# Second product of the score matmuls over 128 rows instead of 64, in a hybrid four-layer decoder step

## The chip, the cores and the metric

The kernel runs on one core of one Trainium2 chip. The metric is the device time of one execution in microseconds (us), as the median over runs of the whole program. A core has a matrix engine (TensorE; "PE" in the profile, its weight loads "PEld"), VectorE ("DVE"), ScalarE ("ACT"), GpSimd ("POOL"), and SyncE ("SP"), which issues most of the DMAs. Each engine works off its own queue in order, and waits for others through semaphores.

## The reference

One inference step of a decoder trunk with four layers, for 512 prompt tokens (one sequence) and 32 sample tokens (8 sequences of 4), width 1024. Every layer is `x = x + mixer(rmsnorm(x)); x = x + conv_ffn(rmsnorm(x))`. The mixers are mLSTM in layers 0 and 3, gated linear attention (GLA) in layer 1, and sliding-window softmax attention with sinks in layer 2. All arrays are float32. What matters here are the two score products of the prompt tokens:

```python
# mLSTM, 8 heads, keys and queries of 64
qk = jnp.einsum('bthd,bshd->btsh', q, k) * w          # w: causal decay
num = jnp.einsum('btsh,bshv->bthv', qk, v) + ...

# softmax attention, 16 query heads on 4 key heads of 64, window 128
s = jnp.einsum('bnqkgd,bnrkd->bnkgqr', q, k) * (HDC ** -0.5)
s = jnp.where(mask[None, :, None, None], s, NEG)
p = jax.nn.softmax(jnp.concatenate([s, sink], axis=-1), axis=-1)[..., :-1]
return jnp.einsum('bnkgqr,bnrkd->bnqkgd', p, v)
```

The rest are projections, the convolutional feed-forward (2816 wide), GLA, the decode paths of the sample tokens, and the new states that are returned.

## The kernel before, in words

**Precision.** Large products are made on operands of the type `F32R` ("fp32r" in the profile). Each operand is split into a high half (a copy to F32R, `hi`) and a low half (`src - hi`, `lo`), and a product is hi·hi + hi·lo + lo·hi. The weights come from HBM in units of up to four 128x128 blocks (`wr`). ScalarE makes `wh` (line 191) and VectorE `wl` (line 192), up to three units or more ahead of use, from a ring of six buffers each.

**Order of the work.** A kernel-wide list of units fixes the order of the projections (`gemm` for outputs with features on partitions, `group` for V). Attention runs beside it as generators (`push`): `gemm` calls `tick` after each 128-row block of its contraction, which lets a generator emit its next piece. So the score products of attention stand in TensorE's queue between the products of the projections. A scheduler behind the program then orders each engine's queue by priority and by estimated readiness, and that order is fixed when the program runs. Nearly every product is issued by the helper `mm` (line 164), so rows of the profile are told apart by their tiles.

**mLSTM scores.** A head has 64 features, and two heads share a tile `Q[p]`, `K[p]` of 128 partitions. `prep(h)` builds for head h three tiles of 128 partitions, `ks`, `qs` and `ql`, one buffer each, where `r` are the 64 rows in which the head lies and `o` the other 64:

- `ks[r]` = high half of k (ScalarE, line 716), `ks[o]` = low half of k (VectorE, 719);
- `qs[r]` and `qs[o]` = high half of q, twice (ScalarE, 717 and 718);
- `ql[r]` = low half of q (VectorE, 720); `ql[o]` is not written.

`scores(h)` then makes for each of four blocks of 128 keys a first product over all 128 rows, `ks·qs` = hi·hi + lo·hi at once, with 512, 384, 256 or 128 query columns, and adds a second one over the 64 rows `r`, hi·`ql`. VectorE multiplies the result by the decay, and `av(h)` uses it. `prep(h + 1)` and the decays of the next head are emitted before `av(h)`, and `scores(h + 1)` after it.

**Softmax scores.** The other way round: here q is split into two halves of the partitions (`qa`, `qb` = tag `qs`: the high half of a head in its own 64 rows, the low half in the other 64; line 1435 on ScalarE, 1436 on VectorE), and k is held twice: `KE` has the high half of the even key head in both halves of the partitions, `KO` that of the odd one (four copies on ScalarE). `KL` has the low half of the even head in rows 0 to 63 and of the odd one in rows 64 to 127 (lines 1418 and 1419 on VectorE). `scores` makes for each of two query blocks a first product over 128 rows, q·`KE` or q·`KO`, and adds one over the 64 rows `hr` of the head, q_hi·`KL`, all with 256 key columns. A head takes 8 products, in two PSUM tiles. Then come the masked maximum (VectorE, line 1472), the exponentials (ScalarE, 1476), the scaling (`normalise`, 1502 on VectorE and 1504 on ScalarE), transposes on TensorE (`transp`, line 167) and the product with V (`pv`).

**The convolution's state.** `ffn` holds its old and new state in a tile `cc` (176 KB are loaded into it at its start, line 424) in the pool of the layer's mixer, with the tag `x1`. The softmax layer's pool also has `kc`, one buffer for the cached keys of the decode path: `load_kc(0)` fills it at the start and `load_kc(1)` again after the first `decode`.

Of the kernel before, what the change touches and what calls it, by code (L numbers as in the profile page):

```python
# [10 lines left out]
F32 = mybir.dt.float32  # L11
F32R = mybir.dt.float32r
I32 = mybir.dt.int32
AF = mybir.ActivationFunctionType
ALU = mybir.AluOpType
AX = mybir.AxisListType
PSUM = bass.MemoryType.PSUM
# [3 lines left out]
NP = 512  # L21
# [9 lines left out]
XW = NF * 34  # L31
# [81 lines left out]
class Step:  # L113
# [35 lines left out]
        self.defer = []  # L149
        self.credit = 0.0  # L150

# [1 line left out]
    def t(self, n=562, p=128, dt=F32):  # L153
        return self.tp.tile([128, 562], dt, tag="t", name="t")[0:p, 0:n]

# [10 lines left out]
    def tr(self, out, in_, k):  # L166
        self.nc.tensor.transpose(out, in_, self.ident[0:k, 0:k])  # L167

# [1 line left out]
    def wdma(self, upto):  # L170
        while self.n_dma < min(upto + 1, len(self.units)):
            u = self.n_dma
# [29 lines left out]
        self.n_use += 1  # L202
        return [(hi[:, i * w:(i + 1) * w], lo[:, i * w:(i + 1) * w]) for i in range(len(kts))]

# [1 line left out]
    def adv(self, q, amount):  # L206
        q[0][1] -= amount
        while q and q[0][1] <= 0:
# [50 lines left out]
        while len(self.defer) > 1:  # L259
            self.adv(self.prio, 1)  # L260

# [1 line left out]
    def gemm(self, mat, kts, c0, hi, lo, evac, off=0):  # L263
        kts = list(kts)
        self.room()
# [83 lines left out]
    def h2(self, ap):  # L349
        return ap.rearrange("p (a b) -> p a b", a=2)  # L350

# [1 line left out]
    def xprep(self, kt, gcol, parts="ab"):  # L353
        nc = self.nc
        x = self.XT[:, kt]
# [59 lines left out]

        self.push(gen(), prio=True, delay=0.01)

# [1 line left out]
    def ffn(self, L, last):  # L419
        nc, a = self.nc, self.a  # L420
        cc = self.mp.tile([128, XW], F32, tag="x1", name="cc")
        cin = cc[:, 0:NF * 16].rearrange("p (f b w) -> p f b w", f=NF, b=NB)
        cout = cc[:, NF * 16:NF * 34].rearrange("p (f x) -> p f x", f=NF)
        nc.sync.dma_start(out=cin, in_=a["fst"][L].rearrange("p (f b w) -> p f b w", f=NF, b=NB))
        rb = self.RB

        def dec(ap):
            return ap.rearrange("p (b x) -> p b x", b=NB)

        for ci, ch in enumerate(CHUNKS):  # L430
            for n, f in enumerate(ch):
                pw = P_CW + (L * NF + f) * 3
                pb = P_CB + L * NF + f
                g = self.t()
                nc.gpsimd.memset(g[:, 0:2], 0.0)
                nc.gpsimd.tensor_copy(dec(g[:, 514:562])[:, :, 0:2], cin[:, f])
                s2 = self.t(T)

                def gate(acc, g=g, s2=s2, f=f, pw=pw, pb=pb):
                    nc.vector.tensor_tensor(out=g[:, 2:274], in0=acc[:, 0, 0:HT], in1=rb[:, 0:HT], op=ALU.mult)  # L440
                    nc.vector.tensor_tensor(out=g[:, 274:514], in0=acc[:, 1, 0:240], in1=rb[:, HT:NP], op=ALU.mult)  # L441
                    nc.vector.tensor_tensor(out=dec(g[:, 514:562])[:, :, 2:6], in0=dec(acc[:, 1, 240:272]), in1=dec(rb[:, NP:T]), op=ALU.mult)  # L442
                    nc.gpsimd.tensor_copy(cout[:, f, 0:2], g[:, 512:514])  # L443
                    nc.gpsimd.tensor_copy(dec(cout[:, f, 2:18]), dec(g[:, 514:562])[:, :, 4:6])
                    c = self.t(560)
                    nc.scalar.activation(c, g[:, 2:562], AF.Identity, scale=self.par[:, pw + 2:pw + 3], bias=self.par[:, pb:pb + 1])  # L446
                    nc.vector.scalar_tensor_tensor(out=c, in0=g[:, 1:561], scalar=self.par[:, pw + 1:pw + 2], in1=c, op0=ALU.mult, op1=ALU.add)
                    nc.vector.scalar_tensor_tensor(out=c, in0=g[:, 0:560], scalar=self.par[:, pw:pw + 1], in1=c, op0=ALU.mult, op1=ALU.add)
                    nc.scalar.activation(c, c, AF.Silu)
                    nc.vector.tensor_tensor(out=s2[:, 0:NP], in0=c[:, 0:NP], in1=rb[:, 0:NP], op=ALU.mult)  # L450
                    nc.vector.tensor_tensor(out=dec(s2[:, NP:T]), in0=dec(c[:, 512:560])[:, :, 2:6], in1=dec(rb[:, NP:T]), op=ALU.mult)

                def up(acc, s2=s2, n=n):
                    h = self.t(T)
                    nc.vector.tensor_tensor(out=self.h2(h), in0=acc[:, :, 0:HT], in1=self.h2(s2), op=ALU.mult)  # L455
                    self.split(self.HH[:, n], self.HL[:, n], h)

                self.gemm(f"fu{L}", range(KT), 128 * f, self.XH, self.XL, gate)
                self.gemm(f"fu{L}", range(KT), 128 * (NF + f), self.XH, self.XL, up)
            fin = ci == len(CHUNKS) - 1  # L460
            for mt in range(6 if last and fin else 8):
                self.gemm(f"fd{L}", ch, 128 * mt, self.HH, self.HL,
                          lambda acc, mt=mt: self.resid(mt, acc, (P_GM + 8 * (L + 1) if not last else None) if fin else -1))
        nc.sync.dma_start(out=a["f_o"][L], in_=cout.rearrange("p f x -> p (f x)"))
# [78 lines left out]
        nc.vector.tensor_scalar(out=u, in0=u, scalar1=1.0 / n, scalar2=EPS, op0=ALU.mult, op1=ALU.add)  # L543
        nc.gpsimd.tensor_tensor(out=u, in0=u, in1=self.half[0:p, 0:cols], op=ALU.pow)  # L544

# [1 line left out]
    def mlstm(self, L, j):  # L547
        nc, a, tc = self.nc, self.a, self.tc
        ctx = ExitStack()
# [161 lines left out]
        def prep(h):  # L711
            r = slice(64 * (h % 2), 64 * (h % 2) + 64)
            o = slice(64 - 64 * (h % 2), 128 - 64 * (h % 2))
            q, k = Q[h // 2][r, 0:NP], K[h // 2][r, 0:NP]
            ks, qs, ql = [mp.tile([128, NP], F32R, tag=x, name=x) for x in ("ks", "qs", "ql")]
            nc.scalar.activation(ks[r], k, AF.Copy)
            nc.scalar.activation(qs[r], q, AF.Copy)
            nc.scalar.activation(qs[o], q, AF.Copy)
            nc.vector.tensor_tensor(out=ks[o], in0=k, in1=ks[r].bitcast(F32), op=ALU.subtract)
            nc.vector.tensor_tensor(out=ql[r], in0=q, in1=qs[r].bitcast(F32), op=ALU.subtract)  # L720
            KQ[h] = (ks, qs, ql, r)

        def scores(h):
            ks, qs, ql, r = KQ.pop(h)
            ws = SW[h]
            s23 = None
            for i in range(4):
                n = NP - 128 * i
                if i < 2:
                    s = self.m()[:, 0:n]  # L730
                elif i == 2:
                    s23 = self.m()
                    s = s23[:, 0:256]
                else:
                    s = s23[:, 256:384]
                self.mm(s, ks[:, i * 128:(i + 1) * 128], qs[:, i * 128:NP], True, False)
                self.mm(s, ks[r, i * 128:(i + 1) * 128], ql[r, i * 128:NP], False, True)
                nc.vector.tensor_tensor(out=ws[i], in0=s, in1=ws[i], op=ALU.mult)

        def hnorm(num, den, ss, em, sc, cols, p, tag):  # L740
            # num: list of PSUM [p, 128], den: SBUF [p, cols]
            nc.vector.scalar_tensor_tensor(out=sc, in0=den, scalar=-1.0, in1=den, op0=ALU.mult, op1=ALU.max)
            nc.vector.tensor_tensor(out=sc, in0=sc, in1=em, op=ALU.max)
            nc.vector.reciprocal(out=sc, in_=sc)
            for c, x in enumerate(num):
                junk = self.junk[0:p, 0:128]
                nc.scalar.activation(junk, x, AF.Square, accum_out=ss[:, c:c + 1])
            nc.vector.tensor_tensor(out=ss, in0=ss, in1=sc, op=ALU.mult)
            nc.vector.tensor_tensor(out=ss, in0=ss, in1=sc, op=ALU.mult)
            self.rms_scale(ss, 128, cols, p)  # L750
            nc.vector.tensor_tensor(out=sc, in0=sc, in1=ss, op=ALU.mult)
# [225 lines left out]
        self.outproj(f"aw{j}", L)  # L977
        return ctx

# [1 line left out]
    def gla(self, L):  # L981
        nc, a, tc = self.nc, self.a, self.tc
        ctx = ExitStack()
# [378 lines left out]
        self.outproj("bw", L)  # L1362
        return ctx

# [1 line left out]
    def swa(self, L):  # L1366
        nc, a, tc = self.nc, self.a, self.tc
        ctx = ExitStack()
# [3 lines left out]
        KF = mp.tile([128, 2, T], F32, name="KF")  # L1372
        KE = mp.tile([128, 2, NP], F32R, name="KE")
        KO = mp.tile([128, 2, NP], F32R, name="KO")
        KL = mp.tile([128, 2, NP], F32R, name="KL")
        KC = {}

        def load_kc(kvp):
# [30 lines left out]
        def kevac(m):  # L1409
            def f(acc):  # L1410
# [4 lines left out]
                nc.scalar.activation(KE[64:128, m], x[0:64, 0:NP], AF.Copy)  # L1415
                nc.scalar.activation(KO[0:64, m], x[64:128, 0:NP], AF.Copy)
                nc.scalar.activation(KO[64:128, m], x[64:128, 0:NP], AF.Copy)
                nc.vector.tensor_tensor(out=KL[0:64, m], in0=x[0:64, 0:NP], in1=KE[0:64, m].bitcast(F32), op=ALU.subtract)
                nc.vector.tensor_tensor(out=KL[64:128, m], in0=x[64:128, 0:NP], in1=KO[64:128, m].bitcast(F32), op=ALU.subtract)
            return f  # L1420

        def qevac(m):
# [30 lines left out]
        def scores(m, par, pr, st):  # L1453
            kvp, g = m // 4, m % 4
            head = (2 * kvp + par) * 4 + g
            q = QS[m][par]
            hr = slice(64 * par, 64 * par + 64)
            ks = KO if par else KE
            s = self.m().rearrange("p (a x) -> p a x", a=2)
            for i in range(2):  # L1460
                blk = 2 * pr + i
                k0 = max(0, blk - 1) * 128
                t0 = blk * 128
                self.mm(s[:, i], q[:, t0:t0 + 128], ks[:, kvp, k0:k0 + 256], True, False)
                self.mm(s[:, i], q[hr, t0:t0 + 128], KL[hr, kvp, k0:k0 + 256], False, True)
            sm = mp.tile([128, 2, 256], F32, tag="smx", name="smx", bufs=6)
            mx, ng, su, es = st
            sink = sk[:, head:head + 1]
# [144 lines left out]
        self.outproj("cw", L)  # L1613
        return ctx

# [1 line left out]
    def run(self):  # L1617
        nc, a = self.nc, self.a
        nc.vector.memset(self.half, -0.5)
# [186 lines left out]
```

## Time and profile before

| | |
|---|---|
| time, median of 3 runs | 2652.68 us (2652.5 to 2652.69) |
| profiled execution: span on the core | 2653.1 us |
| mean granted TensorE clock of the profiled execution | 0.994 of full |
| products (TensorE instructions) | 21303 |
| ScalarE, VectorE instructions | 2096, 3455 |

The span of the profiled execution is its own time; it lies 0.4 us above the median of the other runs. A row of a view of groups reads: line, engine, operation, tile written <- tiles read, shape, x count | busy us, mean ns of one | idle us of the engine before them, and what ended that idle time. For a product the two numbers "128*128" or "64*128" ahead of the shape are the rows and columns of TensorE's array that it uses, and the shape is that of the operand that streams. A row of a view of one tile gives the least, median and largest duration in ns, and the start of the first and the last one in us. A row of the timeline gives start and duration in us, and at its end how many like it are merged. A row of the view by windows gives the stretch, its length, the busy time of PE, PEld, DVE, ACT and POOL with counts, the granted TensorE clock, the DMA engines' busy share and GB/s.

### The profile page before, as it was taken

The numbers are of one execution on the slowest core, as the hardware profiler recorded it, in microseconds if no ns is written. First come the engines' busy times: TensorE is split into PE (matmuls) and PEld (weight loads), VectorE is DVE, ScalarE is ACT, GpSimd is POOL, SyncE is SP. The second block draws the span as 40 slices with busy tenths as digits, with TensorE's granted clock in tenths as the row PEclk, the third lists the DMA queues.
The fourth block names the chain that finished last, engine by engine and source line by source line (L and its number), as shares of the span: only waits on it lengthen the run. The fifth ranks groups of instructions, "written<-read, shape, count | busy, mean of one in ns | idle before, by whom it ended". The sixth has DMA issues, their size and how long they took to land.

```text
span 2653.1 us, 52983 instructions
## 1 busy us (share of the span) xinstructions
PE 2627.2 (99%) x21303; PEld 2535.3 (96%) x21303; DVE 1605.4 (61%) x3455; ACT 1105.3 (42%) x2096; POOL 200.4 (8%) x545
## 2 busy tenths in 40 slices
PE   8999999999999999999999999999999999999998
PEld 8999999999998899999998899999999989999998
DVE  5567765645457667464556666364555676756464
ACT  5444433334455543232346554232345444423232
POOL 1000000001012200000010000000010000000000
PEclk9999999999999999999999999999999999999999
DMA  4332333333222224433331123333233322333332
GB/s 171 95 89 76 85 114 94 91 91 99 76 81 89 87 84 148 138 85 92 107 92 51 53 68 88 88 87 90 85 106 90 85 80 80 102 107 96 89 87 80
DMA packets 136294, 245.16 MB, mean 92 GB/s; under 512 B 16272, under 2 KB 32144, under 8 KB 136016
## 3 DMA queue, kind: packets, MB, share of 16 engines
q1 hardware_dynamic: 134608, 240.16, 30.7%
q8 instruction: 168, 2.75, 0.4%
q10 hardware_dynamic: 1440, 1.60, 0.2%
q14 instruction: 78, 0.64, 0.1%
HBM read 228.80 MB, written 14.94 MB: 92 GB/s over the span
## 4 chain that ended last, share of the span: by engine, by line
PE 96%; DVE 2%; ACT 1%; issue 0%; POOL 0%; DMA 0%; DVEq 0%; SPq 0%; ACTq 0%
PE acc L164 81%; PE m L164 14%; PE m L167 1%; POOL s L544 0%; DVE wl L192 0%; DVE t L513 0%; DMA XT<-in_x 0%; DVE t L1068 0%; ACT wh L191 0%; DVE bc L1047 0%; DVE st L831 0%; ACT smx L1476 0%; DVE t L1072 0%; DVE HL L344 0%; POOL sr L1345 0%
## 5 line engine op out<-in xcount | busy, mean ns | idle before, releaser
L191 ACT ACTIVATE wh<-wr 128x512 fp32r<-128x512 f32 (+2 forms) x776 | 482.6, 623 | 1104.4 <-PE acc L164 1019.3
L164 PE MATMUL acc<-XH,wh 128*128 128x272 f32 x3744 | 789.3, 292 | 0.0
L164 PE MATMUL acc<-XH,wl 128*128 128x272 f32 x3744 | 781.1, 289 | 0.0
L164 PE MATMUL acc<-XL,wh 128*128 128x272 f32 x3744 | 778.0, 289 | 0.0
L192 DVE TENSOR_TENSOR wl<-wr,wh 128x512 fp32r<-128x512 f32 (+2 forms) x776 | 523.4, 675 | 326.0 <-ACT wh L191 322.0
L164 PEld LDWEIGHTS acc<-XH,wh 128*128 128x128 f32 x3744 | 588.5, 189 | 9.8 <-issue 6.1
L164 PEld LDWEIGHTS acc<-XL,wh 128*128 128x128 f32 x3744 | 590.0, 189 | 2.6 <-issue 1.6
L164 PEld LDWEIGHTS acc<-XH,wl 128*128 128x128 f32 x3744 | 588.4, 189 | 2.9 <-issue 1.6
L164 PE MATMUL acc<-HH,wh 128*128 128x272 f32 x1920 | 403.7, 290 | 0.0
L164 PE MATMUL acc<-HH,wl 128*128 128x272 f32 x1920 | 399.4, 288 | 0.0
L164 PE MATMUL acc<-HL,wh 128*128 128x272 f32 x1920 | 399.0, 288 | 0.0
L164 PEld LDWEIGHTS acc<-HH,wh 128*128 128x128 f32 x1920 | 302.1, 188 | 2.3 <-issue 1.0
L164 PEld LDWEIGHTS acc<-HL,wh 128*128 128x128 f32 x1920 | 302.4, 188 | 0.0
L164 PEld LDWEIGHTS acc<-HH,wl 128*128 128x128 f32 x1920 | 301.4, 189 | 0.8 <-issue 0.4
L530 DVE TENSOR_TENSOR XT<-acc,XT 128x544 f32<-128x544 f32 x158 | 114.3, 723 | 142.0 <-PE acc L164 141.0
L443 POOL COPY cc<-t 128x2 f32<-128x2 f32 x88 | 54.6, 621 | 1299.2 <-DVE t L441 1294.0
L440 DVE TENSOR_TENSOR t<-acc,rb 128x272 f32<-128x272 f32 x88 | 38.9, 442 | 142.8 <-PE acc L164 140.1
L164 PE MATMUL m<-wh,XH 128*128 128x256 f32 (+1 forms) x400 | 116.2, 291 | 6.8 <-ACT XH L346 6.4
L164 PE MATMUL m<-wl,XH 128*128 128x256 f32 (+1 forms) x400 | 114.9, 288 | 1.0 <-DVE wl L192 1.0
L164 PE MATMUL m<-wh,XL 128*128 128x256 f32 (+1 forms) x400 | 114.9, 288 | 0.0
L455 DVE TENSOR_TENSOR t<-acc,t 128x544 f32<-128x544 f32 x88 | 63.7, 723 | 68.7 <-PE acc L164 68.1
L446 ACT ACTIVATE t<-t,par 128x560 f32<-128x560 f32 x88 | 75.4, 856 | 50.8 <-DVE t L442 50.8
(342 smaller groups left out, 2664.9 us busy)
## 6 DMA issues: line engine op xcount, KB each, us to landing
wr<-in_w SPq DMA_DIRECT2D x700, 256.0 KB
wr<-in_w SPq DMA_DIRECT2D x64, 192.0 KB
st<-in_a_cs SPq DMA_DIRECT2D x16, 520.0 KB
sd<-in_b_s SPq DMA_DIRECT2D x32, 256.0 KB
out_a_cso<-st SPq DMA_DIRECT2D x8, 520.0 KB
na<-scr SPq DMA_DIRECT2D x16, 256.0 KB
out_b_so<-sd SPq DMA_DIRECT2D x16, 256.0 KB
wr<-in_w SPq DMA_DIRECT2D x12, 272.0 KB
```

The source lines that it names most:

```text
L164: self.nc.tensor.matmul(out, lhsT=lhsT, rhs=rhs, start=start, stop=stop, skip_group_check=True, **kw)
L167: self.nc.tensor.transpose(out, in_, self.ident[0:k, 0:k])
L191: self.nc.scalar.activation(hi[:, 0:n], raw[:, 0:n], AF.Copy)
L192: self.nc.vector.tensor_tensor(out=lo[:, 0:n], in0=raw[:, 0:n], in1=hi[:, 0:n].bitcast(F32), op=ALU.subtract)
L440: nc.vector.tensor_tensor(out=g[:, 2:274], in0=acc[:, 0, 0:HT], in1=rb[:, 0:HT], op=ALU.mult)
L443: nc.gpsimd.tensor_copy(cout[:, f, 0:2], g[:, 512:514])
L446: nc.scalar.activation(c, g[:, 2:562], AF.Identity, scale=self.par[:, pw + 2:pw + 3], bias=self.par[:, pb:pb + 1])
L455: nc.vector.tensor_tensor(out=self.h2(h), in0=acc[:, :, 0:HT], in1=self.h2(s2), op=ALU.mult)
L530: self.nc.vector.tensor_tensor(out=self.h2(x), in0=acc[:, :, 0:HT], in1=self.h2(x), op=ALU.add)
```

## The change

The second product of each pair reads all 128 rows. For that its low half is laid into both halves of the partitions: in mLSTM ScalarE copies `ql[r]` to `ql[o]` (one copy of 64x512 a head); in the softmax layer `KL` is replaced by `KEL` and `KOL`, whose own half VectorE writes as before, and whose other half ScalarE copies (two copies of 64x512 for each of two tiles of key heads). The sums gain the term lo·lo, which was left out. To make room for the additional tile, `cc` takes the tag `kc` in the softmax layer. The numbers and sizes of the products stay, apart from the rows that they read.

```diff
@@ ffn
-        cc = self.mp.tile([128, XW], F32, tag="x1", name="cc")
+        cc = self.mp.tile([128, XW], F32, tag="kc" if L % 3 == 2 else "x1", name="cc")
@@ mlstm, prep
             nc.vector.tensor_tensor(out=ql[r], in0=q, in1=qs[r].bitcast(F32), op=ALU.subtract)
-            KQ[h] = (ks, qs, ql, r)
+            nc.scalar.activation(ql[o], ql[r].bitcast(F32), AF.Copy)
+            KQ[h] = (ks, qs, ql)
@@ mlstm, scores
                 self.mm(s, ks[:, i * 128:(i + 1) * 128], qs[:, i * 128:NP], True, False)
-                self.mm(s, ks[r, i * 128:(i + 1) * 128], ql[r, i * 128:NP], False, True)
+                self.mm(s, ks[:, i * 128:(i + 1) * 128], ql[:, i * 128:NP], False, True)
@@ swa
-        KL = mp.tile([128, 2, NP], F32R, name="KL")
+        KEL = mp.tile([128, 2, NP], F32R, name="KEL")
+        KOL = mp.tile([128, 2, NP], F32R, name="KOL")
@@ swa, kevac
-                nc.vector.tensor_tensor(out=KL[0:64, m], in0=x[0:64, 0:NP], in1=KE[0:64, m].bitcast(F32), op=ALU.subtract)
-                nc.vector.tensor_tensor(out=KL[64:128, m], in0=x[64:128, 0:NP], in1=KO[64:128, m].bitcast(F32), op=ALU.subtract)
+                for hi, lo, src in ((KE, KEL, slice(0, 64)), (KO, KOL, slice(64, 128))):
+                    nc.vector.tensor_tensor(out=lo[src, m], in0=x[src, 0:NP], in1=hi[src, m].bitcast(F32), op=ALU.subtract)
+                nc.scalar.activation(KEL[64:128, m], KEL[0:64, m].bitcast(F32), AF.Copy)
+                nc.scalar.activation(KOL[0:64, m], KOL[64:128, m].bitcast(F32), AF.Copy)
@@ swa, scores
-            hr = slice(64 * par, 64 * par + 64)
-            ks = KO if par else KE
+            ks, kl = (KO, KOL) if par else (KE, KEL)
...
                 self.mm(s[:, i], q[:, t0:t0 + 128], ks[:, kvp, k0:k0 + 256], True, False)
-                self.mm(s[:, i], q[hr, t0:t0 + 128], KL[hr, kvp, k0:k0 + 256], False, True)
+                self.mm(s[:, i], q[:, t0:t0 + 128], kl[:, kvp, k0:k0 + 256], False, True)
```

More of the change, by code (lines that the diff above doesn't have):

```diff
@@ L720, in prep @@
             nc.vector.tensor_tensor(out=ql[r], in0=q, in1=qs[r].bitcast(F32), op=ALU.subtract)
-            KQ[h] = (ks, qs, ql, r)
+            nc.scalar.activation(ql[o], ql[r].bitcast(F32), AF.Copy)
+            KQ[h] = (ks, qs, ql)
         def scores(h):
-            ks, qs, ql, r = KQ.pop(h)
+            ks, qs, ql = KQ.pop(h)
             ws = SW[h]
```

## The prediction

> **What bounds the kernel now.** I read the page first, for the bound, then the tiles of the changed products, then the timeline around them, then the granted clock.
>
> ```profile
> span 2653.1 us, 52983 instructions
> ...
> PE 2627.2 (99%) x21303; PEld 2535.3 (96%) x21303; DVE 1605.4 (61%) x3455; ACT 1105.3 (42%) x2096; POOL 200.4 (8%) x545
> ...
> PE 96%; DVE 2%; ACT 1%; issue 0%; POOL 0%; DMA 0%; DVEq 0%; SPq 0%; ACTq 0%
> ...
> L191 ACT ACTIVATE wh<-wr 128x512 fp32r<-128x512 f32 (+2 forms) x776 | 482.6, 623 | 1104.4 <-PE acc L164 1019.3
> ```
>
> TensorE holds 96% of the chain of waits; VectorE, ScalarE and the DMAs hold almost nothing. The last row shows that the conversion of weights runs as far ahead as its buffers allow: of 1104.4 us that ScalarE sat idle before a conversion, 1019.3 us ended when TensorE finished a product and so freed a buffer. So a microsecond taken from TensorE's own work should come off the end, unless something else then arrives late. A busy TensorE is not one at its peak, though, so next the products that the change touches, one row each from the views of tiles KL, ql and ks:
>
> ```profile
> L164 PE MATMUL m<-KL,qs x64: 379/381/579, 1398.3 to 1532.5; 64*128 64x256 f32 x64
> ```
>
> ```profile
> L164 PE MATMUL m<-ql,ks x64: 322/409/500, 91.2 to 2177.9; 64*128 64x512 f32 x16, 64*128 64x384 f32 x16, 64*128 64x256 f32 x16, 64*128 64x128 f32 x16
> ```
>
> ```profile
> L164 PEld LDWEIGHTS m<-qs,ks x64: 186/187/192, 90.7 to 2177.7; 128*128 128x128 f32 x64
> L716 ACT ACTIVATE ks<-k x16: 610/622/633, 88.8 to 2163.6; 64x512 fp32r<-64x512 f32 x16
> ```
>
> There are 128 such products, 64 in the softmax attention and 64 in the two mLSTM layers, each between products on 128 rows ("64*128" is rows by columns of the array). Their durations overlap in a pipeline; what counts is the distance from start to start. One softmax head:
>
> ```profile
> 1416.10 0.28 PE L164 MATMUL m<-KE,qs 128*128 128x256 f32 x1
> 1416.31 0.39 PE L164 MATMUL m<-KL,qs 64*128 64x256 f32 x1
> 1416.62 0.38 PE L164 MATMUL m<-KE,qs 128*128 128x256 f32 x1
> ...
> 1418.18 0.38 PE L164 MATMUL m<-KL,qs 64*128 64x256 f32 x1
> 1418.49 0.40 PE L164 MATMUL acc<-XL,wh 128*128 128x272 f32 x1
> 1418.73 0.29 PE L164 MATMUL acc<-XH,wl 128*128 128x272 f32 x1
> ```
>
> Against it the projection of V, whose products also read 256 columns, load new weights each time and add up in one PSUM bank, but always on 128 rows (first and last of thirteen starts in a row):
>
> ```profile
> 1385.74 0.28 PE L164 MATMUL m<-wh,XH 128*128 128x256 f32 x1
> ...
> 1387.16 0.28 PE L164 MATMUL m<-wh,XH 128*128 128x256 f32 x1
> ```
>
> Twelve distances in 1.42 us are 0.118 us each, or 0.46 ns a column. In the score run a product takes 0.31 us. The columns, the new weights and the accumulation are the same, so the 0.19 us more goes with the alternation of 128 and 64 rows: TensorE seems to run empty at each alternation, without the next weights loaded ahead. The product after the run pays once more: 0.24 us from 1418.49 to 1418.73, for 272 columns that take 0.126.
>
> **The change, part by part.** *Softmax scores.* A head costs now 1418.49 - 1416.10 = 2.39 us and 0.11 after it, 2.50 in all. With one row mode it is 8 x 0.118 = 0.94. Saved: 1.56 a head, 16 heads: 24.9 us.
>
> *mLSTM scores*, with 512, 384, 256 and 128 columns:
>
> ```profile
> 125.75 0.40 PE L164 MATMUL m<-qs,ks 128*128 128x512 f32 x1
> ...
> 127.24 0.52 PE L164 MATMUL acc<-XH,wh 128*128 128x272 f32 x2
> ...
> 127.97 0.28 PE L164 MATMUL m<-qs,ks 128*128 128x256 f32 x1
> ...
> 128.49 0.39 PE L164 MATMUL acc<-XH,wl 128*128 128x272 f32 x1
> ...
> 129.36 0.22 PE L164 MATMUL m<-qs,ks 128*128 128x128 f32 x1
> ...
> 129.76 0.39 PE L164 MATMUL acc<-XH,wl 128*128 128x272 f32 x1
> ```
>
> The pieces are 1.49 (512 and 384), 0.52 (256) and 0.40 us (128), with 0.11 behind each: 2.74. In one mode, at 0.46 ns a column, 2 x (0.236 + 0.177 + 0.118) = 1.06, and two products on 128 columns. Nothing shows these in this type; they lie between 0.059 by columns and 0.133, which is what seven transposes of 128 columns with full weight loads take at most (0.93 us, row at 1426.01 below). I take 0.09, the middle: 0.18. So 1.24, saved 1.50 a head. In half of the heads the last pair stands beside a product on fewer columns, which stays:
>
> ```profile
> 2177.67 0.33 PE L164 MATMUL m<-qs,ks 128*128 128x128 f32 x1
> 2177.92 0.33 PE L164 MATMUL m<-ql,ks 64*128 64x128 f32 x1
> 2178.18 0.41 PE L164 MATMUL m<-V,t 64*32 64x129 f32 x2
> ```
>
> There only the middle alternation goes; I take 0.2 us off for 8 heads. 16 x 1.50 - 1.6 = 22.4 us.
>
> *The granted clock.* Three stretches of the attention ran at half clock:
>
> ```profile
> 1401.60:1408.30 6.70, 6.70 (x24) 5.58 (x25) 3.03 (x14) 5.20 (x20) 0.00 (x0) 0.50 0.01 2
> 1466.50:1469.80 3.30, 3.30 (x16) 3.30 (x16) 1.59 (x10) 2.19 (x8) 0.00 (x0) 0.50 0.04 16
> 1476.70:1483.40 6.70, 6.70 (x28) 4.42 (x29) 3.52 (x16) 2.46 (x9) 0.64 (x2) 0.50 0.24 70
> ```
>
> All three begin in or just behind a score run (the first follows the double run from 1398.0), where the array streams only a third of the time. Full clock would give back at most half of 16.7 us, 8.4; if density has nothing to do with it, 0; and one new stretch of 6.7 would cost 3.4. Nearest is the kernel's own remainder, dense runs at full clock, so I take 5. The Trainium skill (TensorE: Matmul & The Clock Gate, Part 1) says that half clock follows a window of about 3.4 us of idleness; here TensorE counts as busy throughout, so by that rule's wording these stretches should not be there, and the sum would be 5 us smaller unless the drained array counts as idle.
>
> *Copies on ScalarE.* 16 of ql[o] and 4 of KEL/KOL, 64x512 at 0.622 us (row L716): 12.4 us of ScalarE, which is 42% busy. They are hidden by its idle time, but each waits for a VectorE subtraction at the head of an in-order queue, with weight conversions and exponentials behind it, and the mLSTM scores now wait for it. The tight place is the second head of each mLSTM layer:
>
> ```profile
> 2051.58 0.69 DVE L720 TENSOR_TENSOR ql<-q,qs 64x512 fp32r<-64x512 f32 x1
> ...
> 2052.17 0.39 PE L164 MATMUL m<-qs,ks 128*128 128x512 f32 x1
> ...
> 2052.49 0.50 PE L164 MATMUL m<-ql,ks 64*128 64x512 f32 x1
> ```
>
> ql is ready at 2052.27. The copy brings that to 2052.9 or later, while TensorE, now at 0.236 us for the first product, wants it at 2052.41: 0.5 us late, or some 3 behind other work on ScalarE. Two heads: 1 to 6; I take 1.5, since ScalarE is mostly idle. In the last head ql is 4.0 us early, by the two rows below, and in the heads between by more; there the copy costs nothing. The KEL/KOL copies belong to the projection of K, ahead of that of V (1385.7 above), and the first score comes at 1398.3 (row of KL): covered by V, nothing.
>
> ```profile
> 2167.19 0.69 DVE L720 TENSOR_TENSOR ql<-q,qs 64x512 fp32r<-64x512 f32 x1
> ...
> 2171.87 0.39 PE L164 MATMUL m<-qs,ks 128*128 128x512 f32 x1
> ```
>
> *Softmax behind the scores.* The time from score to transpose shrinks, since a head's and its successor's scores both lie in it, while VectorE and ScalarE need as long as before:
>
> ```profile
> 1423.86 0.90 ACT L1504 ACTIVATE smx<-smx,s 128x256 f32<-128x256 f32 x2
> ...
> 1426.01 0.93 PE L167 MATMUL m<-cst,smx 128*128 128x128 f32 x7
> ```
>
> The probabilities of head 2 are ready 1.25 us before TensorE transposes them; up to 2 x 1.56 us of that distance goes, and some of the chain only waited for TensorE's projections, which come sooner as well. About half of the 16 heads are this close. Between 0 and 1.5 us each, 0 to 12 us; I take 4, since a stall of one head gives slack to the next.
>
> *The moved tile.* The third layer's cc takes the buffer of kc, so its load (issued early today) waits until the last product that reads kc:
>
> ```profile
> L164 PE MATMUL m<-kc,QD x64: 269/269/293, 1452.8 to 1530.0; 64*32 64x128 f32 x64
> ```
>
> ```profile
> L436 POOL COPY t<-cc x6: 195/196/198, 1547.2 to 1629.2; 128x16 f32<-128x16 f32 x6
> ```
>
> That leaves 17 us for 176 KB before GpSimd reads cc, and its result is used later still. Weight loads queued behind it on SyncE are covered by the conversions' lead. Nothing; if the lead failed, 1 to 2 us.
>
> **Sum.** 24.9 + 22.4 + 5 - 1.5 - 4 = 46.8 us. The profiled span is 2653.1, the median of the runs 2652.7, so profile and runs agree: 2606 us. With all bounds good, 24.9 + 22.4 + 8.4 - 0 is 56, or 2597; with 6 and 12 of stalls and no gain in clock it is 29, or 2624.
>
> **The rivals.**
> 1. *Given back in the softmax.* VectorE and ScalarE keep their pace, and TensorE waits at most transposes. For it: 1.25 us of slack against 3.1 us taken. Against: their share of the span, 61% and 42%. Up to 25 us of the softmax saving goes: 2618 to 2640.
> 2. *No change.* The 0.19 us belongs to something other than rows. A rule of that kind: a weight load overlaps a running product only if their row groups differ. Then each of the eight products of a head would take 0.118 and its load of 0.187 (row of LDWEIGHTS), 2.44 us against 2.50 now, and mLSTM heads 1.24 + 8 x 0.187 = 2.74 against 2.74: 2652. The rule is from the Trainium skill (TensorE: Matmul & The Clock Gate, Part 3). Against it: thirteen starts on one row group at 0.118.
> 3. *Slower.* ScalarE stands at a copy, waiting for VectorE's subtraction behind queued work, and the scores behind it wait. There are 18 such places (16 heads, 2 kv tiles). The gains less the softmax stalls are 24.9 + 22.4 + 5 - 4 = 48.3 us, so the point at which it turns is 2.7 us of TensorE's time at each place; at 4 us it would be 2677. For it: the order of each queue is static. Against: only two heads have slack under half a microsecond, and conversions run ahead.
> 4. *More than forecast.* No stall and a clock that stays full: 2588 to 2597.
>
> **How the numbers follow.** Forecast (2597 to 2618) 0.72; rival 1 0.15; rival 2 0.04; rival 3 0.05; rival 4 0.04. 0.2%, 5.3 us, is about what a measurement can tell from no change. Faster is forecast, 1 and 4: 0.91; same 0.04; slower 0.05. The range 2597 to 2624 holds the forecast and about half of rival 1: 0.8.
>
> **What the profile after would show.** Score products 0.12 us apart at 256 columns, no 64-row products in m<-KL or m<-ql, and the run of a softmax head under 1 us; the same count of instructions on PE, 20 more on ACT; the clock at 1.00 in the attention; PE's waits for ql, KEL or smx of a few microseconds at most. Wrong it would be if the distances stay at 0.3 with 128 rows, or if PE's idle time grows by over 15 us, with releasers ACT ql or ACT smx.

## The result, and the profile after

The changed kernel takes 2605.8 us in the median (2602.7 to 2607.7, four runs) against 2652.7 us before; the ratio is 0.982, with a 95% interval of 0.9806 to 0.9833. The span of its profiled execution is 2605.9 us, 47.2 less than before.

The page of the changed kernel has the same count of products, and TensorE still holds the chain of waits:

```profile
span 2605.9 us, 53001 instructions
...
PE 2577.6 (99%) x21303; PEld 2519.6 (97%) x21303; DVE 1603.1 (62%) x3455; ACT 1115.7 (43%) x2116; POOL 200.5 (8%) x545
...
PE 96%; DVE 2%; ACT 1%; issue 0%; POOL 0%; DMA 0%; DVEq 0%; SPq 0%; ACTq 0%
...
L191 ACT ACTIVATE wh<-wr 128x512 fp32r<-128x512 f32 (+2 forms) x776 | 482.4, 623 | 1063.6 <-PE acc L164 967.7
```

TensorE's busy time fell by 50 us without one product less, ScalarE has 20 instructions more, and its conversions still wait for TensorE. The views of the tiles KEL and ql show the second products on the whole array, and the copy:

```profile
L164 PE MATMUL m<-KEL,qs x32: 274/280/283, 1389.9 to 1485.9; 128*128 128x256 f32 x32
```

```profile
L164 PE MATMUL m<-ql,ks x64: 272/310/500, 91.5 to 2130.8; 128*128 128x512 f32 x16, 128*128 128x384 f32 x16, 128*128 128x256 f32 x16, 128*128 128x128 f32 x16
L721 ACT ACTIVATE ql<-ql x16: 627/631/634, 84.8 to 2122.0; 64x512 fp32r<-64x512 f32 x16
```

The softmax head whose start stood in the prediction, in the timeline (start, duration):

```profile
1401.70 0.28 PE L164 MATMUL m<-KE,qs 128*128 128x256 f32 x1
1401.82 0.28 PE L164 MATMUL m<-KEL,qs 128*128 128x256 f32 x1
...
1402.64 0.28 PE L164 MATMUL acc<-XL,wh 128*128 128x272 f32 x1
1402.76 0.29 PE L164 MATMUL acc<-XH,wl 128*128 128x272 f32 x1
```

Eight products take 0.94 us instead of 2.39, and the product behind them 0.12 instead of 0.24. The weight loads (PEld) show what changed between two products. Before, a load started together with its own product, behind the one ahead of it:

```profile
1417.24 0.19 PEld L164 LDWEIGHTS m<-KE,qs 128*128 128x128 f32 x1
1417.24 0.38 PE L164 MATMUL m<-KE,qs 128*128 128x256 f32 x1
```

After, it starts 0.11 us ahead of its product, as the product before it starts (at 1402.06):

```profile
1402.06 0.19 PEld L164 LDWEIGHTS m<-KE,qs 128*128 128x128 f32 x1
1402.17 0.28 PE L164 MATMUL m<-KE,qs 128*128 128x256 f32 x1
```

And an mLSTM head, the same as before:

```profile
124.17 0.40 PE L164 MATMUL m<-qs,ks 128*128 128x512 f32 x1
...
124.99 0.42 PE L164 MATMUL acc<-XH,wh 128*128 128x272 f32 x2
...
125.62 0.35 PE L164 MATMUL m<-qs,ks 128*128 128x256 f32 x1
125.81 0.28 PE L164 MATMUL m<-ql,ks 128*128 128x256 f32 x1
125.93 0.29 PE L164 MATMUL acc<-XH,wl 128*128 128x272 f32 x1
...
126.68 0.33 PE L164 MATMUL m<-qs,ks 128*128 128x128 f32 x1
126.84 0.28 PE L164 MATMUL m<-ql,ks 128*128 128x128 f32 x1
126.95 0.34 PE L164 MATMUL acc<-XH,wl 128*128 128x272 f32 x1
127.13 0.41 PE L164 MATMUL acc<-XH,wh 128*128 128x272 f32 x2
```

Its pieces are now 0.82, 0.31 and 0.27 us (1.49, 0.52 and 0.40 before), with 0.05 behind the last one: 1.45 instead of 2.74.

Where the 47.2 us lie is best read by layer, since the order of the projections is the same in all kernels here. The table gives the time from one projection product to another: around the attention of layer 0, from ahead of the softmax layer to behind it, and around the attention of layer 3 (worked out from the starts of the 190th, 460th, 3200th, 3520th, 4640th and 5110th product that reads `wl`). Half clock is the granted clock's record inside the softmax layer.

| kernel | median of runs, us | layer 0 | softmax layer | layer 3 | half clock in it |
|---|---|---|---|---|---|
| before | 2652.7 | 157.6 | 206.1 | 231.0 | 17.1 |
| changed | 2605.8 | 148.5 | 176.3 | 221.9 | 3.4 |
| softmax only | 2621.9 | 157.5 | 174.4 | 231.0 | 0 |
| mLSTM only | 2634.4 | 148.5 | 207.8 | 221.9 | 20.5 |
| copies, 64 rows | 2653.0 | 157.6 | 204.5 | 231.0 | 13.7 |
| grouped | 2621.4 | 149.7 | 189.1 | 223.2 | 6.8 |
| grouped, two banks | 2626.0 | 152.1 | 189.9 | 225.6 | 3.4 |
| changed, again | 2602.7 | 148.5 | 174.8 | 221.9 | 0 |
| zero halves | 2604.0 | 148.2 | 176.0 | 221.6 | 3.4 |
| wide last pair (one run) | 2601.5 | 148.2 | 174.4 | 221.6 | 0 |
| zero halves and hnd | 2598.9 | 147.0 | 174.4 | 220.1 | 0 |
| and norms | 2599.4 | 147.0 | 176.0 | 220.0 | 3.4 |

The change gained 9.1 us in each mLSTM layer and 29.8 in the softmax layer; 0.8 was lost elsewhere (0.4 ahead of layer 0's attention, 0.4 between it and the softmax layer). The mLSTM columns repeat to 0.1 us. The softmax column has two sources: with one row mode it is 174.4 to 174.8 at full clock and 176.0 to 176.3 with one stretch of 3.4 us at half clock; with alternating rows it goes 204.5, 206.1, 207.8 with four, five and six such stretches. So 3.4 us at half clock cost 1.6 us, and at full clock the old scores would give 206.1 - 5 x 1.6 = 198.1; that is an estimate, since no profile here has alternating rows at full clock throughout. By it, 198.1 - 174.6 = 23.5 of the 29.8 us belong to the rows and 6.3 to the clock. Two executions are far slower than all others of their kernels and stand in no comparison: 3548 us with the copies on 64 rows and 5712 us of the kernel before.

### The profile page after: what moved, and what is told of

It is laid out like the page before. It is cut to its first block, busy times and chain, and to the rows that moved or that the text cites. A ratio compares the mean times of both kernels' runs of the same rounds, so it can differ in the third digit from the quotient of the medians.

```text
span 2605.9 us, 53001 instructions
## 1 busy us (share of the span) xinstructions
PE 2577.6 (99%) x21303; PEld 2519.6 (97%) x21303; DVE 1603.1 (62%) x3455; ACT 1115.7 (43%) x2116; POOL 200.5 (8%) x545
## 4 chain that ended last, share of the span: by engine, by line
PE 96%; DVE 2%; ACT 1%; issue 0%; POOL 0%; DMA 0%; DVEq 0%; SPq 0%; ACTq 0%
PE acc L164 82%; PE m L164 13%; PE m L167 1%; POOL s L544 0%; DVE wl L192 0%; DVE t L513 0%; DMA XT<-in_x 0%; ACT wh L191 0%; DVE t L1069 0%; DVE t L700 0%; DVE ks L719 0%; DVE bc L1048 0%; DVE ql L720 0%; DVE st L832 0%; ACT smx L1479 0%
```

## Experiments

Theory R: each alternation between products on 128 and on 64 rows costs TensorE some 0.2 us, and nothing else in the change counts. P: it is the moved tile, the copies or the new order of the queues. S: a product on 64 rows is slow by itself.

**One half at a time.** Softmax only: `prep` and `scores` of mLSTM as before. mLSTM only: `swa` and `ffn` as before, with

```diff
+            nc.scalar.activation(ql[o], ql[r].bitcast(F32), AF.Copy)
...
-                self.mm(s, ks[r, i * 128:(i + 1) * 128], ql[r, i * 128:NP], False, True)
+                self.mm(s, ks[:, i * 128:(i + 1) * 128], ql[:, i * 128:NP], False, True)
```

> The change in the softmax layer alone; mLSTM as before (64 rows, no copy of ql). Theory R (each alternation between products on 128 and on 64 rows costs some 0.2 us, and nothing else of the change counts): the 29.8 us that the changed kernel gained in the softmax layer stay, the 18.2 of the two mLSTM layers go, so 2623 us (2620 to 2627), score products of the softmax 0.118 us apart and those of mLSTM as before, and about 3.4 us or nothing at half clock in the softmax layer. Rival P (the gain comes from the moved tile, the copies or the new order of the queues): the gain doesn't follow the layers; all of it or none would be here, 2606 or 2653. Rival S (a product on 64 rows is slow by itself, whatever stands beside it) expects the same as R.

> The change in the two mLSTM layers alone; softmax layer as before, cc in its old place. R: 18.2 us gained, 2634.5 us (2632 to 2637), three stretches at half clock in the softmax layer as before, 6 to 8 us of its gain absent with them. P: 2653, since the moved tile is out, or 2606. S: as R.

Measured: 2621.9 us (ratio 0.9888, 0.9872 to 0.9905) and 2634.4 us (0.9933, 0.9918 to 0.9948). The gain follows the layers, to 0.1 us in the mLSTM columns; P is out as a whole. The rows of the windows view from 1385 to 1545 us, softmax only and then mLSTM only (the clock is the third number from the end):

```profile
1385.00:1545.00 160.00, 159.86 (x1429) 150.80 (x1428) 124.30 (x360) 112.32 (x300) 9.10 (x19) 1.00 0.24 71
```

```profile
1385.00:1545.00 160.00, 159.88 (x1161) 133.80 (x1160) 103.24 (x324) 95.87 (x272) 7.91 (x18) 0.94 0.16 48
```

In the same 160 us TensorE starts 268 products more, and ScalarE and VectorE keep up. With one row mode the layer has no half clock in this profile; with alternating rows it has 20.5 us of it, where 17.1 us (three stretches as before) were expected.

**The copies without the rows.**

```diff
-                self.mm(s, ks[:, i * 128:(i + 1) * 128], ql[:, i * 128:NP], False, True)
+                self.mm(s, ks[r, i * 128:(i + 1) * 128], ql[r, i * 128:NP], False, True)
...
-                self.mm(s[:, i], q[:, t0:t0 + 128], kl[:, kvp, k0:k0 + 256], False, True)
+                self.mm(s[:, i], q[hr, t0:t0 + 128], kl[hr, kvp, k0:k0 + 256], False, True)
```

> All that the change adds stays (copies of ql, KEL and KOL, the moved tile), but the second products read only the 64 rows of the head, as before. R: the gain is gone, 2653 us (2651 to 2657); what lies above 2652.7 is the price of the copies. P: 2606, since all but the rows is there. S: 2653.

Measured: 2653.0 us, ratio 1.0001 (0.9992 to 1.0011). No price or gain of the copies and the moved tile can be told, and both mLSTM columns stand where they did (157.6 and 231.0); the rows make the effect.

**Grouping.** In the kernel before, two first products stand together and then two second ones, still on 64 rows (the softmax part; mLSTM likewise):

```diff
                 self.mm(s[:, i], q[:, t0:t0 + 128], ks[:, kvp, k0:k0 + 256], True, False)
+            for i in range(2):
...
                 self.mm(s[:, i], q[hr, t0:t0 + 128], KL[hr, kvp, k0:k0 + 256], False, True)
```

> The kernel before, second products still on 64 rows, but two first products stand together and then two second ones (softmax: both query blocks of a PSUM tile; mLSTM: key blocks 0 and 1, then 2 and 3). So there are half as many alternations with the same products. R: about half of the gain on scores, 0.78 us a softmax head (12.5) and 0.7 us an mLSTM head (11), plus 0 to 4 us of clock: 2627 us (2621 to 2633), with 0.12 us between two products of a kind and 0.31 at the alternations. S: 2653, since the same 64-row products run. P: 2653.

Measured: 2621.4 us (0.9883, 0.9868 to 0.9898). The steps were not the 0.12 and 0.31 us expected: the median is 0.223 us between two products of a kind and 0.21 at an alternation. Two sums stand open in one PSUM bank in this kernel, and its scores are other than the reference's; it is read for its time alone. To keep the sums right and to see whether the bank mattered, the second grouping pairs products whose sums lie in different banks:

> The grouping once more (two first products, then two second ones on 64 rows, from the kernel before), now with the two open sums in different PSUM banks: in the softmax layer the two tiles of a head go together, in mLSTM the last key block has a tile of its own. R: as the first grouping, 2621 us (2617 to 2627), with 0.21 and 0.22 us from start to start by turns (0.1 for running empty ahead of an alternation, 0.1 for the weights behind it). S: 2653. If sharing a bank had made the first grouping fast, this one would stand at 2653 too.

Measured: 2626.0 us (0.9896, 0.9879 to 0.9913). A softmax head of the second grouping, in the timeline, where "x2" is two products in a row:

```profile
1406.75 0.47 PE L164 MATMUL m<-KE,qs 128*128 128x256 f32 x2
1407.15 0.50 PE L164 MATMUL m<-KL,qs 64*128 64x256 f32 x2
1407.59 0.50 PE L164 MATMUL m<-KE,qs 128*128 128x256 f32 x2
1408.02 0.50 PE L164 MATMUL m<-KL,qs 64*128 64x256 f32 x2
1408.45 0.39 PE L164 MATMUL acc<-XL,wh 128*128 128x272 f32 x1
```

Two products now take 0.43 us, 0.22 each, where alternating ones take 0.31 and unmixed ones 0.12. In this profile the median distance from a 64-row product to another one is 0.223 us and from there back to 128 rows 0.206, so an alternation has two parts: the last product of one kind is followed 0.1 us late, and the first of the next kind, whose weights are loaded only as it starts, is followed 0.1 us late once more. Single products between alternations pay both. A 64-row product is not slow by itself: from one 64-row product to another the step is 0.223 us, and from one 128-row product to another in the same groups it is 0.223 as well; S is out. The softmax column agrees: halfway between 198.1 and 174.6 lies 186.4, and the first grouping without its two half-clock stretches comes to 189.1 - 3.2 = 185.9. The second one stands at 189.9 - 1.6 = 188.3, since the scheduler put four of the heads back into alternation in part. Its mLSTM columns gained 5.5 us instead of 7.8, because there it left only the first two key blocks grouped; the bank has no part in this that the runs show. In mLSTM the first grouping got 7.8 of 9.1 us, more than the half expected; 1.6 of them stand at the steps behind products on fewer columns (st and V).

**The copies left out.** The other half is zero instead, written once a layer; for room, Ac and Wc are put into unused columns of Z:

```diff
+            nc.scalar.activation(QL[n][o], qz[o, 0:NP], AF.Copy)
...
-            ks, qs, ql = [mp.tile([128, NP], F32R, tag=x, name=x) for x in ("ks", "qs", "ql")]
...
+            ql = QL[h % 2]
...
-            nc.scalar.activation(ql[o], ql[r].bitcast(F32), AF.Copy)
```

> The changed kernel unaltered, for comparison with the two kernels beside it: 2602 to 2608 us, as its four runs so far. If the spread of its runs comes from the granted clock, its profile has between 0 and 7 us at half clock in the softmax layer, and a time to match, about 1.5 us more for each 3.4 us.

> The changed kernel without its copies: the other half of ql, KEL and KOL is zero, written once a layer ahead of use (ql in two fixed tiles, one for even heads and one for odd), so the second product on 128 rows adds lo*0; the rows Ac and Wc move into unused columns of Z for room. R: the rows make the gain, so it stays, and TensorE's waits for the copy of ql (1.1 us in two waits in the profile of the changed kernel, 0.8 us each in the length of the run) go: 2604 us, 1 to 2 below the changed kernel run beside it. Rival (the copies cost more than their waits show, since ScalarE stands 13.7 us waiting for VectorE's ql): 3 to 8 us below. If values mattered (lo*lo) nothing would change in time.

Measured: 2602.7 us (2602.4 to 2606.8) for the changed kernel and 2604.0 us (2602.8 to 2607.3) with zero halves; no difference that can be told. In the mLSTM columns 0.25 us a layer are gained, not 0.8. The reason shows at the second head of layer 0, first in the changed kernel:

```profile
97.86 0.69 DVE L720 TENSOR_TENSOR ql<-q,qs 64x512 fp32r<-64x512 f32 x1
...
98.17 0.56 PE L164 MATMUL m<-qs,ks 128*128 128x512 f32 x2
...
98.58 0.63 ACT L721 ACTIVATE ql<-ql 64x512 fp32r<-64x512 f32 x1 [0.67 <-DVE ql L720]
...
99.26 0.67 PE L164 MATMUL m<-ql,ks 128*128 128x512 f32 x2 [0.53 <-ACT ql L721]
```

and then with zero halves:

```profile
93.81 0.69 DVE L724 TENSOR_TENSOR ql<-q,qs 64x512 fp32r<-64x512 f32 x1
```

```profile
94.09 0.40 PE L164 MATMUL m<-qs,ks 128*128 128x512 f32 x1
94.56 0.49 PE L164 MATMUL m<-ql,ks 128*128 128x512 f32 x1
```

Without the copy VectorE's own subtraction (ready at 94.50) is the next to be late: the first four products take 1.15 us instead of 1.61, where 0.81 is what other heads need. Of the 0.46 gained there, 0.2 goes again at the next pair (256 columns), which takes 0.34 us instead of 0.24 and comes 0.12 later behind its neighbour. In the changed kernel the scheduler had put two first products ahead of the wait for the copy, which hid part of it already.

**The same rule at other places.** The mLSTM decode rows (hnd) are transposed on 128 rows, with zeros below:

```diff
-            hn = mp.tile([64, 132], F32, tag="hnd", name="hnd")[:, 0:129]
+            hf = mp.tile([128, 132], F32, tag="hnd", name="hnd")
+            nc.gpsimd.memset(hf[64:128, 0:128], 0.0)
...
-            self.tr(td[:, 0:64], HND[p], 64)
+            self.tr(td[:, 0:128], HND[p], 128)
```

> As the kernel with zero halves, and the same rule at another place: the 16 transposes of the mLSTM decode rows (hnd, 64 rows, between transposes and products on 128 rows) read 128 rows, the lower 64 being zeros from GpSimd. In the changed kernel the steps into, at and out of them are 0.203, 0.202 and 0.23 us, where products on 128 rows take about 0.11, 0.11 and 0.125. R: 16 x 0.29 = 4.7 us less than the kernel with zero halves, 2599 to 2600. S: the middle step alone, 16 x 0.09 = 1.5 us. A rival that the wait for hnd's values ends last there: no change, since TensorE would stand there as long.

Measured: 2598.9 us (2597.6 to 2601.4; 0.9792, 0.9778 to 0.9806), the shortest median here. Its layers gained 1.3 and 1.6 us over the kernel with zero halves, 2.8 together instead of 4.7. A transpose with the products behind it, first in the changed kernel and then here:

```profile
119.38 0.27 PE L167 MATMUL m<-cst,hnd 64*128 64x64 f32 x1
119.58 0.52 PE L164 MATMUL acc<-XH,wh 128*128 128x272 f32 x2
119.94 0.41 PE L164 MATMUL acc<-XL,wh 128*128 128x272 f32 x2
```

```profile
118.00 0.27 PE L167 MATMUL m<-cst,hnd 128*128 128x128 f32 x1
118.03 0.49 PE L164 MATMUL acc<-XH,wh 128*128 128x272 f32 x2
118.36 0.41 PE L164 MATMUL acc<-XL,wh 128*128 128x272 f32 x2
```

At 14 of the 16 places the steps into, at and out of the transpose went from 0.203, 0.202 and 0.232 us to 0.109, 0.028 and 0.210, which is the 0.29 forecast, differently shared. At the other two the transpose stands at the wait for hnd, as the rival has it, and nothing was gained. The two columns hold 13 of the 14 places, 3.8 us, so 1.0 was lost again in them: the steps into the first products of the score pairs are 0.7 us longer in all and those into products with V 0.3. The wait behind the first of these is the one shown with the last pair below.

On top of that the norm's small products, which had 32 rows:

```diff
-                self.mm(b1[:, 0:ND], self.oner[0:ND], dgs[i][0:ND, NP:T], i == 0, i == 1)
+                self.mm(b1[:, 0:ND], self.oner, dgs[i][:, NP:T], i == 0, i == 1)
```

> As the kernel with zero halves and hnd on 128 rows, and the rule at one more place: the product that spreads the sample tokens' norm factors (32 rows, twice in each of 8 norms) reads 128 rows, of which 96 are zeros that the same VectorE instruction writes. Now the steps are 0.322, 0.133, 0.188 and 0.230 us, where 128-row products would take 0.23, 0.11, 0.11 and 0.15 or so. R: 8 x 0.27 = 2.2 us less than the kernel with hnd, so 2596 to 2598. Rival: the wait for the factors ends last at this place, and nothing changes.

Measured: 2599.4 us (0.9795, 0.9779 to 0.981), the same as without. The steps themselves went as expected, from 0.873 to 0.582 us at each norm, and the stretches between the three columns of the table are 2.0 us shorter together (0.9, 0.6 and 0.5). But 2.3 us in all are less than what a stretch or two at half clock take from one execution to the next; this kernel's profile has one in the softmax layer, the other's none.

**The last pair of an mLSTM head.**

```diff
+                c = min(i, 2) * 128
...
+                self.mm(s, ks[:, i * 128:(i + 1) * 128], ql[:, c:NP], False, True)
```

> The changed kernel, but the last pair of an mLSTM head reads 256 query columns instead of 128 (the first 128 sums are not used). In the changed kernel this pair and the product behind it start 0.163, 0.112 and 0.178 us apart, 0.453 together, where by columns it would be 0.059, 0.059 and 0.125. Theory L (a product shorter than the load of the next weights waits for them): twice the columns cost 0.118, 0.118 and 0.125, so 0.361, that is 0.09 us less a head where a projection stands behind. Rival C (a fixed cost of these sums, or of their place in the row of products): 0.05 us more for each product, 0.55 together. The whole time moves by less than 1 us either way.

Measured: 2601.5 us, a single run.

```profile
123.69 0.38 PE L164 MATMUL m<-qs,ks 128*128 128x256 f32 x1
123.91 0.28 PE L164 MATMUL m<-ql,ks 128*128 128x256 f32 x1
124.03 0.28 PE L164 MATMUL acc<-XH,wl 128*128 128x272 f32 x1
124.15 0.41 PE L164 MATMUL acc<-XH,wh 128*128 128x272 f32 x2
```

The three distances are 0.22, 0.12 and 0.12, together 0.46, against 0.45 with half the columns. Neither number was met. Twice the columns cost 0.01 us instead of 0.12, as L says of products shorter than the next weights' load; but the first of the pair is 0.1 us late whatever its width, as C has it. The traces show what that 0.1 us is. VectorE multiplies the scores of the key block before (L740 here, L739 in the changed kernel), and the first weight load of the pair carries a wait for VectorE:

```profile
123.21 0.43 DVE L740 TENSOR_TENSOR t<-m,t 128x256 f32<-128x256 f32 x1
123.69 0.19 PEld L164 LDWEIGHTS m<-qs,ks 128*128 128x128 f32 x1
```

The multiplication ends at 123.63, the load starts 0.05 us later, together with its product, and the second product follows 0.22 us behind the first. In the kernel with hnd on 128 rows the same multiplication ends at 125.08, the load at 125.14 is 0.09 us ahead of its product, and at 128 columns the second product follows 0.07 us behind it, where it takes 0.16 in the changed kernel. In the changed kernel six of the sixteen last pairs stand so, and some pairs on 256 columns in part; eight others stand behind products on fewer rows or columns.

## Why the prediction was right

The total came out as forecast, 46.8 us against 47.2 between the profiles (46.9 between the medians), and the mechanism is the one named. That it came so close is luck: the term for the softmax behind the scores was 4.0 us too low and the clock 1.3, against 2.7 and 1.4 too much for the mLSTM and softmax scores and 0.8 lost where the sum had no term.

- *Softmax scores*, 24.9 us: 23.5 by the estimate at full clock, stalls included. The price by the neighbouring 128-row products at 0.118 us was the right row.
- *The clock*, 5: 6.3 by the same estimate. The profile before has five stretches of 3.4 us in the softmax layer, that of the changed kernel one, its second profile none. The size depends on the execution: the kernel before took 2646.9 us at a mean clock of 0.997 and 2658.3 at 0.993 in executions beside the experiments. The reason given, the thin score runs, holds in part. In the mLSTM-only kernel a stretch begins at 1392.5 us behind sixteen alternating products alone; but two of the three stretches of the kernel before had products of the decode path ahead of their score run, and the one of the changed kernel begins at 1449.7, behind 36 decode products on 16 or 128 columns from 1446.48 on. The wording of the Trainium skill's rule (TensorE: Matmul & The Clock Gate, Part 1: half clock after a window of idleness) holds only if such thin stretches count as idle: TensorE shows as busy in all of those in the softmax layer.
- *Softmax behind the scores*, -4: mis-sized. The slack did shrink, but not below nothing. Where it is about smallest, ScalarE's last part ends just ahead of the transposes:

```profile
1422.16 0.89 ACT L1507 ACTIVATE smx<-smx,s 128x256 f32<-128x256 f32 x2
...
1423.11 0.93 PE L167 MATMUL m<-cst,smx 128*128 128x128 f32 x7
```

  That is 0.06 us, and the transposes' total in this layer is the same 12.5 us before and after. The step that failed is the count of both heads' 1.56 us against a chain that was taken to move little. At the head that the prediction showed, 9.91 us lay between its first score (1416.10) and its transposes (1426.01) before; now it is 7.20, from 1401.70 to the transposes here:

```profile
1407.87 0.68 DVE L1505 TENSOR_TENSOR smx<-smx,s 128x512 f32<-128x512 f32 x1
...
1408.90 0.27 PE L167 MATMUL m<-cst,smx 128*128 128x128 f32 x1
```

  The probabilities, though, are ready 6.85 us behind the first score instead of 8.66. So 2.7 us were taken between score and transposes, and 1.8 of them from the chain itself; the slack went from 1.25 to 0.35. That the chain had been waiting for TensorE's projections in that time is argued from the order of the work, not shown. The list of TensorE's waits in the changed kernel names no smx and only this of the copies:

```profile
PE m L164 <- ACT ql L721: 1.1, 2, 0.5
```

- *mLSTM scores*, 22.4: 18.2, with the second heads' stall in it. That stall was 1.61 - 0.82 = 0.8 us a layer, 1.6 together, where 1.5 stood. So the products gave 19.8. The term that was too large is the pair on 128 columns: 0.453 us with the product behind it, where 2 x 0.09 + 0.125 = 0.305 was assumed, and the 256-column pair is 0.31 in some heads instead of 0.24. The prediction priced these products with their weights loaded ahead; the traces show that here the load waits for VectorE's multiplication of the block before (0.05 us from its end to the load, above), and the price is the same 0.1 us of weights not loaded ahead.
- *Copies and moved tile*, nothing: confirmed by the kernel that has them without the rows. The load of cc went to its new time, and GpSimd read it 15 us later, in the changed kernel:

```profile
1493.61 0.33 SPq L424 DMA_DIRECT2D cc<-in_fst  x1
```

```profile
L436 POOL COPY t<-cc x9: 192/193/199, 1509.1 to 1627.1; 128x16 f32<-128x16 f32 x9
```

Of the rivals, the give-back in the softmax and the slower ScalarE queue both had their place in the profile (0.06 us of slack; 13.7 us in twelve waits of ScalarE at the copies of ql, 0.67 of them in the row above), and TensorE lost no more than the 1.1 us by it. "No change" by weights that load ahead only across different row groups is refuted: the products of the changed kernel all use the same 128 rows and follow at 0.12 us, with each load started while the product ahead runs; it is the change of rows that keeps the weights back.

## What to carry to other kernels

Where a product on 64 or 32 rows stands between products on all 128, filling the missing rows with something harmless (zeros, or a term that was left out) took about 0.2 us off each change of rows here, for a copy on an engine that was waiting anyway; where rows can't be filled, put products of one kind together. Not every smaller number of rows costs that. In the kernel before, most of the products on 96 rows (V with t, in the new states of mLSTM and GLA) follow and are followed without delay:

```profile
320.47 0.41 PE L164 MATMUL acc<-XH,wl 128*128 128x272 f32 x2
320.73 0.41 PE L164 MATMUL m<-V,t 96*128 96x260 f32 x2
320.97 0.41 PE L164 MATMUL acc<-XH,wh 128*128 128x272 f32 x2
```

The 64 steps from 128 rows into such products have a median of 0.125 us, for 272 columns that take 0.125 anyway; one of them is as high as 0.182. The 64 steps back have a median of 0.121, but 14 of them, all in GLA, take 0.19 to 0.225, and why was not followed. The Trainium skill (TensorEngine Tiling (Array Packing), Key Properties) says that changing the tiling mode drains the engine, and the runs agree for the change between 128 and 64 rows and give the price: 0.1 us until the first product of the next kind can start, and 0.1 us of weights not loaded ahead. Read start-to-start distances for this: TensorE was "99% busy" with it and without it.

## What the runs showed of the hardware that was not expected

- Half clock followed stretches in which the profile counts TensorE as busy but its products have few columns or alternate in rows, and each 3.4 us of it cost 1.6 us. No threshold comes out of these runs: by an estimate (columns of the products started, at 0.46 ns each), the array streamed for 0.24 to 0.63 of the 3.4 us ahead of the stretches in the softmax layer, and other 3.4 us with 0.35 to 0.6 were followed by full clock. What decides stays open.
- A similar stretch at 56 to 58 us, during the start and behind a wait of 2.3 us, is 0, 3.4 or 6.8 us long from one kernel's profile to the next, and moves all that follows: the first column of the table begins at 83.3 us in one and at 87.4 us in another, with the same program up to there but for a few copies. Single terms below 2 us are read from distances in a stage, not from the time of a run.
- Going from 128 to 64 columns costs nothing when the product stands at the default place: in the changed kernel the 27 steps from V's products into the sample tokens' 64-column ones have a median of 0.119 us. Into 64-column products that are given a place in the array (st behind the scores) the step is 0.203 us.
- A weight load that waits for another engine is not started ahead either, and costs the same 0.1 us, though no idle time of TensorE shows it.
